# A hybrid decoder block on one core: gate and up products made ahead are looked up by the main loop, and the end of the mixing stage is reordered

## The chip, the cores and the metric

One core of one Trainium2 chip runs the whole block in one launch. The metric is device microseconds (us) of a run. All data is float32. A matrix product in full precision is made of three matmuls here: each operand is split into a rounded part and the rest, and three of the four cross products are added in PSUM.

## What is computed

The reference is one residual layer with two halves. The part that matters here, cut from it:

```
x = x + gt_m * (concat(attention(h), mlstm(h)) @ w_out)      # h = modulate(rms_norm(x))
h = modulate(rms_norm(x, g_ffn), sh_f, sc_f)
x = x + gt_f * ((silu(h @ w_gate) * (h @ w_up)) @ w_down)    # 1024 tokens, width 1024, D_FF = 2816
```

## The kernel before

The program is written as one long list of operations, and a scheduler fixes each engine's order when it is built. Its stages are: loads and norms ("init", "start"), the input projection ("vm", "min"), a stage with the attention and the output projection w_out ("at", "mm"), the gate and up projections ("gu"), and the down projection ("dn"). PE is TensorE, DVE VectorE, ACT ScalarE, POOL GpSimd, SP the queue that issues the DMAs.

**Gate and up.** D_FF is cut into 22 slices of 128. A pass f of the loop over slices makes the gate and the up result of one slice for all 1024 tokens, by a 2x2 scheme with seven products P1 to P7 instead of eight. One product contracts half the width: 4 tiles of 128, three matmuls each, 12 matmuls of 128x128 by 128x512, in `mm3_on` (L1052, L1053, L1054). So a pass has 84. P1 (weights: first half of the gate slice, operand A11) goes to a PSUM bank "g" and is copied out by ACT (L1138, into `q[:, 0]`); P2 (second half, operand A12) is added to it in the same bank, which gives the gate result, and ACT takes its silu into `q[:, 1]`. The five others go to banks "s" (`gu_pss`) and "t" (`gu_pst`). Their weights are sums of gate and up weights: `weights` makes them on POOL from two loaded buffers `rawgu` (L1115 t1, L1116 t2, L1121 t3, L1125 t4), and every product's weights are then split by ACT (the cast L242) and DVE (the subtract L243) into `gu_wt`, of which there are seven buffers. There are two buffers `rawgu`, so the pair for the next slice is loaded when the pair before has been read. The operands A22, S1 to S4 are sums over the normed tokens, made once by `sums` on DVE and POOL.

**Products made ahead.** A11 and A12 need only one half of the tokens each to be ready, so P1 and P2 of the slices 0 to 5 are made already while the attention stage ends (`first_two`, weights by `gate_weights` L1068): 144 matmuls, named `mm_psg<-mm_slab,mm_slab` or `mm_psg<-mm_slab,mm_s` with the lines L1052 to L1054 in the trace. Each result pair q is put in a dictionary `early`. The loop is meant to find it there. But `early` is a name of the enclosing function, and the same function binds it a second time before the stage runs, to the list of later token projections:

```
early = {}                                       # with first_two
...
early = [tok_body(...) for w in LATER.split()]   # L1351
...
        if f not in early:                       # weights, L1112, and gate_up
            got["P1"] = parts(g[:, 0])
```

The inner functions look the name up when they run. They find a list of seven entries: `early[f] = q` stores into it, and no slice number f is ever found in it. So the loop makes P1 and P2 again for all 22 slices.

**The end of the attention stage.** `drive` interleaves three streams, the projections "mm", the attention "at" and its inputs "qn", by rates. The last entry of "mm" is `tail`: the output projection of the column groups 2 and 3 (attention; 4 to 7 are the mLSTM heads) for the first half of the tokens (`last_out`, half 0), the norm and the transposition of that half (`h2_half`, L1004 on PE, L1005 on ACT), the weights and products of slices 0 and 1; then, when the attention's last results are there, the output projection for the second half of the tokens (groups 0 to 3, L155 to L157; L952 adds it to the residual), its norm and transposition, the other products ahead, and `sums`. The PSUM of this stage has two banks "g" and three "t".

**POOL's other work.** In even passes, `down_sums` (L1172 to L1176, four sums on POOL) makes sums of w_down and stores them for the down stage; in odd passes, `spill` (L1184 to L1187, four sums on POOL, seven stores) stores the results of two passes. Buffers of one size, the slabs, serve nearly everything; there are 39 (`NSLAB`).

Of the kernel before, what the change touches and what calls it, by code (L numbers as in the profile page):

```python
# [44 lines left out]
WM, WA, WL, WQ, R2 = 220, 140, 66, 28, 1.2  # L45
GA = (0, 0, 2, 3, 9, 18, 22, 24)

DOWN_AHEAD = 5
TWICE = 8
# [16 lines left out]
def hymba_block(ctx, tc, x, vecs, gate_bias, w_in, w_out, w_gu, w_down, w_ada_m, w_ada, b_ada,  # L66
# [1000 lines left out]
    def gate_weights(fs, tile=None):  # L1067

        for f in fs:
            got = []  # L1070
            raw = raws.tile([P, 2, HALF], F32, tag="raw", name=f"rawg{f}")
            nc.sync.dma_start(raw, w_gu[f, :, 0].rearrange("p (k n) -> p k n", k=2))
            h, l = ((tile or slab)([2, 4, P], FR) for _ in range(2))
            split(h.rearrange("p a k n -> p a (k n)"), l.rearrange("p a k n -> p a (k n)"), raw)
            gates_w[f] = [[(h[:, a, i], l[:, a, i]) for i in range(4)] for a in range(2)]

# [24 lines left out]
    def weights(pool, f, raw):  # L1101

        g, u = raw
        tt = nc.gpsimd.tensor_tensor

        def parts(src):
            w = work(pool, "wt", [2, 4, P], FR, bufs=7)
            split(w[:, 0].rearrange("p k n -> p (k n)"), w[:, 1].rearrange("p k n -> p (k n)"), src)
            return [(w[:, 0, i], w[:, 1, i]) for i in range(4)]

        got = {}
        if f not in early:  # L1112
            got["P1"] = parts(g[:, 0])
        t1, t2, t3 = (work(pool, "tr", [HALF], bufs=3) for _ in range(3))
        tt(t1, u[:, 0], g[:, 0], op=OP.subtract)  # L1115
        tt(t2, u[:, 1], t1, op=OP.subtract)  # L1116
        got["P6"] = parts(t2)
        got["P5"] = parts(t1)
        if f not in early:
            got["P2"] = parts(g[:, 1])  # L1120
        tt(t3, u[:, 1], u[:, 0], op=OP.subtract)  # L1121
        got["P7"] = parts(t3)
        got["P3"] = parts(u[:, 1])
        t4 = work(pool, "tr", [HALF], bufs=3)
# [192 lines left out]
    def tail(pool):  # L1317
# [30 lines left out]
    with tc.tile_pool(name="awork", bufs=1) as pool:  # L1348
        btab = slab([T])
        nc.sync.dma_start(btab, mask_tab)  # L1350
        early = [tok_body(("qk" if w[0] == "q" else "va") + w[1], raw_qk if w[0] == "q" else raw_v, int(w[1]),  # L1351
                          tuple(int(hf) for hf in w[2:])) for w in LATER.split()]
        items = early + [w_out_body([4, 5], (0, 1), True, ()), w_out_body([6, 7], (0,), False, ()),
# [8 lines left out]
        drive(("mm", after(chain(items), tail(pool)), WM), ("at", after(*att), WA), ("qn", after(*pre), WQ))  # L1362
        tick(99)
    open_psum("psum_f", s=3, t=2)
    with tc.tile_pool(name="fwork", bufs=1) as pool:
        lab[0] = "gu"
        raw = load_gu(0)
        w = weights(pool, 0, raw)
        for f in range(NF):
# [10 lines left out]
            else:  # L1380
                down_sums(f // 2)
# [77 lines left out]
```

## Time and profile before

| | |
|---|---|
| median of 3 runs | 1355.57 us (1353.12 to 1358.3) |
| the profiled execution | 1357.78 us, its span 1355.6 us |
| mean granted TensorE clock over the span | 0.988 |
| PE busy | 1306.1 us, 96% of the span |
| DVE, ACT, POOL busy | 65%, 43%, 40% |

The time of an execution is its span, from the first to the last instruction in the trace, and the little that lies around it, here 2.2 us. A matmul's row shows its start and its modelled length; matmuls overlap, so the distance of two starts is what one costs, not its length. An idle time in brackets stands in the row of the instruction that came after it, with the engine and line that ended it. The granted clock is given as a share of full speed.

### The profile page before, as it was taken

The page shows a single profiled execution, that of the slowest core. Times are in us where ns is not written, and L with a number is a line of the kernel's source. Part 1 is how long each engine was busy: PE and PEld are TensorE (multiplying, and loading weights), DVE is VectorE, ACT ScalarE, POOL GpSimd, SP SyncE. Part 2 cuts the span into 40 slices and gives each one's busy share as a digit, 9 for nine tenths or more (in the row PEclk, how much of TensorE's full clock was granted, in tenths as well). Part 3 has the DMA queues.
Part 4 walks back from the last instruction along what each step waited for, and adds up shares of the span by engine and source line. Part 5 has one row for each costly group of instructions (what it writes and reads, how often), then busy time and mean ns, then how long its engine had stood idle before and what let it go on. Part 6 is the DMA issues. An engine that isn't in the chain of part 4 may idle for free.

```text
span 1355.6 us, 18979 instructions
## 1 busy us (share of the span) xinstructions
PE 1306.1 (96%) x6983; PEld 1093.5 (81%) x6983; DVE 879.2 (65%) x1465; ACT 581.3 (43%) x1098; POOL 536.2 (40%) x417
## 2 busy tenths in 40 slices
PE   5999999999999999996979999999999999999998
PEld 5897888899899877775767888888888888888886
DVE  6837956973666698994367565556665555665575
ACT  5423444444565565556253233333332333644341
POOL 5401301333333385411154666766676573002121
PEclk9899999999999999997999999999999999999999
DMA  9134223532121132111112444344445436927564
GB/s 367 65 105 140 66 91 102 163 126 69 41 63 32 48 113 90 32 62 63 63 63 101 163 163 148 142 169 163 151 154 176 149 141 224 387 103 246 197 233 140
DMA packets 68579, 180.07 MB, mean 133 GB/s; under 512 B 7620, under 2 KB 7876, under 8 KB 68486
## 3 DMA queue, kind: packets, MB, share of 16 engines
q1 hardware_dynamic: 68486, 178.85, 38.3%
q8 instruction: 55, 0.90, 0.3%
q14 instruction: 38, 0.31, 0.1%
HBM read 138.72 MB, written 40.11 MB: 132 GB/s over the span
## 4 chain that ended last, share of the span: by engine, by line
PE 86%; DVE 6%; ACT 3%; issue 2%; DMA 2%; POOL 1%; SPq 0%; ACTq 0%; DVEq 0%; POOLq 0%
PE gu_pss L1053 6%; PE gu_pss L1054 6%; PE gu_pss L1052 6%; PE mm_psg L155 4%; PE mm_psg L156 4%; PE mm_psg L157 4%; PE min_psg L157 4%; PE min_psg L156 4%; PE min_psg L155 4%; PE gu_psg L1054 3%; PE gu_psg L1053 3%; PE gu_psg L1052 3%; PE at_psv L835 2%; PE at_pss L800 2%; PE dn_pss L1052 2%; PE dn_pss L1054 2%
## 5 line engine op out<-in xcount | busy, mean ns | idle before, releaser
L243 DVE TENSOR_TENSOR gu_wt<-gu_tr,gu_wt 128x512 fp32r<-128x512 f32 x88 | 87.3, 1011 | 88.6 <-ACT gu_wt L242 88.2
L1053 PE MATMUL gu_pss<-mm_slab,gu_wt 128*128 128x512 f32 x352 | 139.9, 397 | 3.6 <-DVE mm_slab L243 3.6
L1054 PE MATMUL gu_pss<-mm_slab,gu_wt 128*128 128x512 f32 x352 | 139.3, 396 | 0.0
L1052 PE MATMUL gu_pss<-mm_slab,gu_wt 128*128 128x512 f32 x352 | 138.6, 394 | 0.0
L242 ACT CAST gu_wt<-gu_tr 128x512 fp32r<-128x512 f32 x88 | 54.5, 622 | 189.4 <-POOL gu_tr L1116 107.4
L243 DVE TENSOR_TENSOR gu_wt<-rawgu,gu_wt 128x512 fp32r<-128x512 f32 x66 | 71.8, 1088 | 34.4 <-ACT gu_wt L242 34.2
L243 DVE TENSOR_TENSOR dn_wt<-dn_slab,dn_wt 128x512 fp32r<-128x512 f32 x72 | 53.1, 737 | 48.4 <-ACT dn_wt L242 47.2
L1053 PEld LDWEIGHTS gu_pss<-mm_slab,gu_wt 128*128 128x128 f32 x352 | 66.6, 189 | 21.1 <-DVE mm_slab L243 5.7
L157 PE MATMUL min_psg<-start_slab,min_slab 128*128 128x512 f32 x192 | 78.2, 407 | 0.8 <-DVE min_slab L243 0.8
L1052 PEld LDWEIGHTS gu_pss<-mm_slab,gu_wt 128*128 128x128 f32 x352 | 66.5, 189 | 15.5
L1054 PEld LDWEIGHTS gu_pss<-mm_slab,gu_wt 128*128 128x128 f32 x352 | 66.5, 189 | 15.1
L155 PE MATMUL min_psg<-start_slab,min_slab 128*128 128x512 f32 x192 | 77.1, 402 | 0.0
L156 PE MATMUL min_psg<-start_slab,min_slab 128*128 128x512 f32 x192 | 77.1, 402 | 0.0
L242 ACT CAST dn_wt<-dn_slab 128x512 fp32r<-128x512 f32 x72 | 44.7, 621 | 69.3 <-PE dn_pss L1054 29.4
L1245 POOL TENSOR_TENSOR dn_slab<-dn_slab,dn_slab 128x512 f32<-128x512 f32 x12 | 17.8, 1499 | 140.2 <-DVE dn_slab L1244 139.5
L156 PE MATMUL mm_psg<-mm_slab,start_slab 128*128 128x256 f32 x256 | 73.1, 286 | 0.0
L157 PE MATMUL mm_psg<-mm_slab,start_slab 128*128 128x256 f32 x256 | 73.0, 286 | 0.0
L155 PE MATMUL mm_psg<-mm_slab,start_slab 128*128 128x256 f32 x256 | 72.9, 286 | 0.0
L1053 PE MATMUL gu_psg<-mm_slab,gu_wt 128*128 128x512 f32 x176 | 69.4, 394 | 0.0
L1054 PE MATMUL gu_psg<-mm_slab,gu_wt 128*128 128x512 f32 x176 | 69.4, 394 | 0.0
L1052 PE MATMUL gu_psg<-mm_slab,gu_wt 128*128 128x512 f32 x176 | 69.2, 393 | 0.0
L809 ACT ACTIVATE at_s<-at_s,at_mins 128x128 f32<-128x128 f32 (+7 forms) x64 | 49.4, 777 | 41.6 <-DVE at_mins L803 21.0
(377 smaller groups left out, 3972.0 us busy)
## 6 DMA issues: line engine op xcount, KB each, us to landing
rawgu<-in_w_gu_dram SPq DMA_DIRECT2D x44, 512.0 KB, 4.4
pd<-gu_slab SPq DMA_DIRECT2D x77, 256.0 KB, 2.1
dn_slab<-pd SPq DMA_DIRECT2D x72, 256.0 KB, 5.3
ada_slab<-in_w_ada_dram SPq DMA_DIRECT2D x32, 512.0 KB, 4.4
gu_slab<-in_w_down_dram SPq DMA_DIRECT2D x22, 512.0 KB, 6.3
td<-gu_slab SPq DMA_DIRECT2D x22, 512.0 KB, 2.6
dn_slab<-td SPq DMA_DIRECT2D x44, 256.0 KB, 5.4
init_slab<-in_w_ada_m_dram SPq DMA_DIRECT2D x16, 512.0 KB, 10.2
```

Of the source, the lines that this page charges most:

```text
L155: mm(o, a[0], b[0], start=start, stop=False)
L156: mm(o, a[0], b[1], start=False, stop=False)
L157: mm(o, a[1], b[0], start=False, stop=stop)
L242: nc.scalar.copy(dst_h, src)
L243: (eng or nc.vector).tensor_tensor(dst_l, src, dst_h.bitcast(F32), op=OP.subtract)
L800: mm(o[:, e, 0:w], q[r, qi, cols], k[ch][r, ki, 0:w], start=qi == ki, stop=qi > ki)
L809: nc.scalar.activation(s[e][:, 0:n], s[e][:, 0:n], AF.Exp, bias=mins[e][:, 0:1], scale=-1.0, accum_out=z)
L835: mm(pv[:, e, P if short else 0:256], v[kb // 4][:, kb % 4, e, :], h[:, j * 256:j * 256 + (P if short else 256)], start=kb == 0 and i == 0 ...
L1052: mm(o, a[0], b[0], start=start, stop=False, skip_group_check=more)
L1053: mm(o, a[0], b[1], start=False, stop=False, skip_group_check=more)
L1054: mm(o, a[1], b[0], start=False, stop=stop, skip_group_check=more)
L1245: nc.gpsimd.tensor_tensor(y, y, xr, op=OP.add)
```

## The change

The diff, nearly whole. The list of projections gets a name of its own, so that `early` stays the dictionary. `FIRST` is 6: for slices under 6 `weights` makes no parts for P1 and P2, and `gate_up` takes q out of `early`.

```diff
-WM, WA, WL, WQ, R2 = 220, 140, 66, 28, 1.2
+WM, WA, WL, WQ, R2 = 220, 140, 66, 28, 1.1
+FIRST = 6
...
-    def gate_weights(fs, tile=None):
+    def gate_weights(fs):
         for f in fs:
...
-            h, l = ((tile or slab)([2, 4, P], FR) for _ in range(2))
+            h, l = (slab([2, 4, P], FR) for _ in range(2))
...
+            yield 0.05
...
-        if f not in early:
+        if f >= FIRST:
             got["P1"] = parts(g[:, 0])
...
-        if f not in early:
+        if f >= FIRST:
             got["P2"] = parts(g[:, 1])
...
-    def tail(pool):
+    all4 = [0, 1, 2, 3]
+
+    def tail():
 
         ws = w_out_load([2, 3])()()
         kept.update(ws)
-        w67 = {k: kept.pop(k) for k in (6, 7)}
-        yield from last_out([2, 3], ws, 0, ((2, 0), (3, 0)), (rest(w67),))
-        gate_weights((0, 1))
-        begun, rest_ = first_two((0, 1)), [first_two((2, 3)), first_two((4, 5))]
-        all4 = [0, 1, 2, 3]
-        wait = tuple((p, 1) for p in range(4))
-        while not all(v in done for v in wait):
+        yield from rest({k: kept.pop(k) for k in (6, 7)})
+        yield from last_out([2, 3], ws, 0, ((2, 0), (3, 0)), (gate_weights((0, 1)),))
+        while not all((p, 1) in done for p in range(4)):
             yield next(begun, None)
-        gate_weights((2, 3), lambda shape, dt: work(pool, "s", shape, dt, bufs=NS))
-        left = next(begun, None)
-        if left is None:
-            begun = rest_.pop(0)
-        yield from last_out(all4, {k: kept.pop(k) for k in all4}, 1, (), (begun,))
-        gate_weights((4, 5))
-        for g in rest_:
-            yield from g
+
+    begun = None
+
+    def second_half(pool):
+        w = {}
+
+        def ahead():
+            for _ in gate_weights((4, 5)):
+                pass
+            yield
+            w.update(weights(pool, 0, load_gu(0)))
+            yield
+
+        ws = {k: kept.pop(k) for k in all4}
+        tiles = w_out_tiles(all4, ws, 1, False)
+        for _ in gate_weights((2, 3)):
+            pass
+        bg.append(ahead())
+        xn = []
+        for t in tiles:
+            xn.append(normed(t))
+            tick()
+        for g in (begun, first_two((2, 3)), h2_half(1, xn), first_two((4, 5))):
+            for _ in g:
+                pass
         sums()
+        return w
...
-        early = [tok_body(...
+        later = [tok_body(...
...
+        begun = first_two((0, 1))
-        drive(("mm", after(chain(items), tail(pool)), WM), ("at", after(*att), WA), ("qn", after(*pre), WQ))
+        drive(("mm", after(chain(items), tail()), WM), ("at", after(*att), WA), ("qn", after(*pre), WQ))
         tick(99)
     open_psum("psum_f", s=3, t=2)
     with tc.tile_pool(name="fwork", bufs=1) as pool:
+        lab[0] = "mm"
+        w = second_half(pool)
         lab[0] = "gu"
-        raw = load_gu(0)
-        w = weights(pool, 0, raw)
+        summed = 0
         for f in range(NF):
...
             if f % 2:
                 spill(f // 2)
-            else:
-                down_sums(f // 2)
+            while f >= FIRST and summed * (NF - FIRST) < (f + 1 - FIRST) * (NF // 2):
+                down_sums(summed)
+                summed += 1
```

In words: the projection tiles of the groups 6 and 7 for the second half (48 matmuls) come before the last projection of the first half instead of behind it; the gate weights of slices 0 and 1 are made inside the norm of that half; the last output projection runs after the attention stage is closed, with the next stage's PSUM (three banks "s", two "t" instead of three "t"), followed by the products of slices 2 and 3, the transposition of the second half, the products of slices 4 and 5, and the sums; the weights of slice 0 are made while that projection runs. The sums of w_down, one set in each even pass before, are made in 11 of the 16 passes from f = 6 on: 6, 7, 8, 10, 11, 13, 14, 16, 17, 19, 20.

Three places show how the engines' orders move. In the changed file the lines after L47 stand two further down (L1052 is L1054 there, L1004 is L1006).

PE where the attention stage ends, before: the last transpositions of the first half of the tokens, then the first product ahead (slice 0, one bank).

```order
L1004 MATMUL mm_pst_6841<-ident,mm_slab_6415 128x128
L1004 MATMUL mm_pst_6841<-ident,mm_slab_6473 128x128
L1004 MATMUL mm_pst_6841<-ident,mm_slab_6537 128x128
L1052 MATMUL mm_psg_6877<-mm_slab_6793,mm_slab_6855 128x512
L1053 MATMUL mm_psg_6877<-mm_slab_6793,mm_slab_6855 128x512
L1054 MATMUL mm_psg_6877<-mm_slab_6793,mm_slab_6856 128x512
L1052 MATMUL mm_psg_6877<-mm_slab_6811,mm_slab_6855 128x512
```

The same place after:

```order
L1006 MATMUL mm_pst_6757<-ident,mm_slab_6668 128x128
L1054 MATMUL mm_psg_6833<-mm_slab_6733,mm_slab_6707 128x512
L1054 MATMUL mm_psg_6872<-mm_slab_6733,mm_slab_6713 128x512
L1055 MATMUL mm_psg_6833<-mm_slab_6733,mm_slab_6707 128x512
L1056 MATMUL mm_psg_6833<-mm_slab_6733,mm_slab_6708 128x512
L1055 MATMUL mm_psg_6872<-mm_slab_6733,mm_slab_6713 128x512
L1056 MATMUL mm_psg_6872<-mm_slab_6733,mm_slab_6714 128x512
L1006 MATMUL mm_pst_6763<-ident,mm_slab_6503 128x128
L1006 MATMUL mm_pst_6763<-ident,mm_slab_6559 128x128
L1006 MATMUL mm_pst_6763<-ident,mm_slab_6618 128x128
```

Before, all transpositions came first and the products of slice 0 alone followed. After, the products of two slices (banks 6833 and 6872) stand between the transpositions, tile by tile; the attention's last transpositions and readout (L824, L837) come after them.

ACT in a pass of the loop, before (slice 1): copy of P1, seven weight casts, copy of P5, two silu.

```order
L1138 COPY gu_slab_7534<-gu_psg_7535 128x512
L242 CAST gu_wt_7637<-rawgu_0_7530 128x512
L1146 COPY gu_slab_7550<-gu_pss_7566 128x512
L1063 ACTIVATE gu_slab_7534<-gu_psg_7535 128x512
L242 CAST gu_wt_7645<-gu_tr_7641 128x512
L242 CAST gu_wt_7648<-gu_tr_7640 128x512
L242 CAST gu_wt_7651<-rawgu_0_7530 128x512
L242 CAST gu_wt_7655<-gu_tr_7642 128x512
L242 CAST gu_wt_7658<-rawgu_1_7532 128x512
L242 CAST gu_wt_7663<-gu_tr_7661 128x512
L1063 ACTIVATE gu_slab_7550<-gu_slab_7550 128x512
```

A pass after (slice 2):

```order
L244 CAST gu_wt_7679<-gu_tr_7675 128x512
L244 CAST gu_wt_7682<-gu_tr_7674 128x512
L244 CAST gu_wt_7686<-gu_tr_7676 128x512
L1148 COPY gu_slab_7600<-gu_pss_7616 128x512
L244 CAST gu_wt_7689<-rawgu_1_7597 128x512
L244 CAST gu_wt_7694<-gu_tr_7692 128x512
L1065 ACTIVATE gu_slab_7600<-gu_slab_7600 128x512
```

In the passes 0 to 5 the copy and the silu of the bank "g" and the two casts from the first buffer `rawgu_0` are gone. On PE the products of `gu_psg` go from 528 matmuls to 384 over the whole loop, so 144 fewer; the products ahead stay 144. POOL and SP have as many instructions as before.

POOL in one pass, before, from the sum behind P7 of slice 1 to that of slice 2 (L1152 marks a pass): the spill of the slices 0 and 1 among the weight sums t1 to t4; the first sum of `down_sums` comes in the next pass, behind the last row.

```order
L1115 TENSOR_TENSOR gu_tr_7789<-rawgu_1_7681,rawgu_0_7679 128x512
L1185 TENSOR_TENSOR gu_slab_7667<-gu_slab_7551,gu_slab_7666 128x512
L1186 TENSOR_TENSOR gu_slab_7666<-gu_slab_7405,gu_slab_7551 128x512
L1116 TENSOR_TENSOR gu_tr_7790<-rawgu_1_7681,gu_tr_7789 128x512
L1121 TENSOR_TENSOR gu_tr_7791<-rawgu_1_7681 128x512
L1187 TENSOR_TENSOR gu_slab_7667<-gu_slab_7551,gu_slab_7667 128x512
L1125 TENSOR_TENSOR gu_tr_7810<-rawgu_0_7679,gu_tr_7790 128x512
L1152 TENSOR_TENSOR gu_slab_7700<-gu_slab_7698,gu_slab_7699 128x512
L1172 TENSOR_TENSOR gu_slab_7815<-gu_slab_7815 128x512
L1173 TENSOR_TENSOR gu_slab_7815<-gu_slab_7816,gu_slab_7815 128x512
```

After, a pass with both, shown from its third row to its end (L1154, slice 6) and one row on:

```order
L1187 TENSOR_TENSOR gu_slab_8318<-gu_slab_8202,gu_slab_8317 128x512
L1188 TENSOR_TENSOR gu_slab_8317<-gu_slab_8056,gu_slab_8202 128x512
L1118 TENSOR_TENSOR gu_tr_8451<-rawgu_1_8342,gu_tr_8450 128x512
L1123 TENSOR_TENSOR gu_tr_8452<-rawgu_1_8342 128x512
L1189 TENSOR_TENSOR gu_slab_8318<-gu_slab_8202,gu_slab_8318 128x512
L1174 TENSOR_TENSOR gu_slab_8330<-gu_slab_8330 128x512
L1127 TENSOR_TENSOR gu_tr_8471<-rawgu_0_8340,gu_tr_8451 128x512
L1175 TENSOR_TENSOR gu_slab_8330<-gu_slab_8331,gu_slab_8330 128x512
L1177 TENSOR_TENSOR gu_slab_8331<-gu_slab_8331,gu_slab_8330 128x512
L1178 TENSOR_TENSOR gu_slab_8331<-gu_slab_8331 128x512
L1154 TENSOR_TENSOR gu_slab_8361<-gu_slab_8359,gu_slab_8360 128x512
L1174 TENSOR_TENSOR gu_slab_8476<-gu_slab_8476 128x512
```

Before, four sums of the spill or four of `down_sums` stood in a pass beside its own five, nine in all. After, the four of `down_sums` (now L1174, L1175, L1177, L1178) and the four of the spill (L1186 to L1189, the first just ahead of the rows shown) stand in one, thirteen in all, and one of them goes ahead of t4 (L1127).

## Rows read from the trace of the kernel before

**Rows 1.** The page: span, and busy time of two engines.

```profile
span 1355.6 us, 18979 instructions
PE 1306.1 (96%) x6983; PEld 1093.5 (81%) x6983; DVE 879.2 (65%) x1465; ACT 581.3 (43%) x1098; POOL 536.2 (40%) x417
```

**Rows 2.** Busy us by stretch: PE, PEld, DVE, ACT, POOL, clock, DMA share, GB/s.

```profile
620.00:630.00 10.00, 3.49 (x17) 1.83 (x15) 6.63 (x11) 9.66 (x16) 0.00 (x0) 0.83 0.00 1
630.00:640.00 10.00, 6.32 (x16) 4.74 (x16) 3.58 (x3) 4.83 (x8) 1.68 (x2) 0.67 0.54 166
...
700.00:710.00 10.00, 7.23 (x31) 5.22 (x29) 10.00 (x9) 7.55 (x15) 8.69 (x6) 1.00 0.30 105
...
1000.00:1020.00 20.00, 20.00 (x88) 16.22 (x88) 13.79 (x15) 6.23 (x11) 14.35 (x10) 1.00 0.42 164
```

**Rows 3.** Line L1052 by tile: count, duration ns min/median/max, first and last start.

```profile
L1052 PE MATMUL gu_psg<-mm_slab,gu_wt x176: 388/393/402, 703.1 to 1128.2; 128*128 128x512 f32 x176
...
L1052 PE MATMUL mm_psg<-mm_slab,mm_slab x32: 389/395/795, 628.8 to 702.2; 128*128 128x512 f32 x32
...
L1052 PE MATMUL mm_psg<-mm_slab,mm_s x16: 388/393/796, 670.1 to 691.1; 128*128 128x512 f32 x16
```

**Rows 4.** Timeline of PE, products ahead at full clock: start, length, what.

```profile
691.77 0.40 PE L1052 MATMUL mm_psg<-mm_slab,mm_slab 128*128 128x512 f32 x1
...
702.63 0.39 PE L1054 MATMUL mm_psg<-mm_slab,mm_slab 128*128 128x512 f32 x1
```

**Rows 5.** Timeline of PE, idle times in brackets, end of the attention stage.

```profile
621.41 1.32 PE L1004 MATMUL mm_pst<-ident,mm_slab 128*128 128x128 f32 x8 [1.10 <-ACT mm_slab L1005]
623.78 0.66 PE L1004 MATMUL mm_pst<-ident,mm_slab 128*128 128x128 f32 x4 [1.05 <-ACT mm_slab L1005]
628.79 0.80 PE L1052 MATMUL mm_psg<-mm_slab,mm_slab 128*128 128x512 f32 x1 [4.35 <-ACT mm_slab L242]
...
637.77 0.79 PE L1052 MATMUL mm_psg<-mm_slab,mm_slab 128*128 128x512 f32 x1 [3.65 <-ACT mm_slab L1085]
...
638.79 0.63 PE L1054 MATMUL mm_psg<-mm_slab,mm_slab 128*128 128x512 f32 x1
639.22 0.63 PE L1052 MATMUL mm_psg<-mm_slab,mm_slab 128*128 128x512 f32 x1
```

**Rows 6.** The same view, from the second half's transpositions into the loop.

```profile
684.58 0.80 PE L1052 MATMUL mm_psg<-mm_slab,mm_s 128*128 128x512 f32 x1 [3.51 <-ACT mm_slab L1085]
...
706.70 0.50 PE L1053 MATMUL gu_pss<-mm_slab,gu_wt 128*128 128x512 f32 x1 [0.67 <-DVE mm_slab L243]
...
710.08 0.50 PE L1053 MATMUL gu_pss<-mm_slab,gu_wt 128*128 128x512 f32 x1 [2.18 <-DVE mm_slab L243]
...
711.78 0.77 PE L1053 MATMUL gu_pss<-mm_slab,gu_wt 128*128 128x512 f32 x1 [0.74 <-DVE mm_slab L243]
```

**Rows 7.** Timeline of ACT before the first product ahead, and at its copy.

```profile
625.31 1.46 ACT L1005 ACTIVATE mm_slab<-mm_pst,modf 128x512 f32<-128x512 f32 x2
...
627.67 2.01 ACT L242 CAST mm_slab<-rawg 128x1024 fp32r<-128x1024 f32 x2
...
633.91 1.04 ACT L242 CAST mm_s<-rawg 128x1024 fp32r<-128x1024 f32 x1 [4.23 <-DMA rawg<-in_w_gu_dram]
```

**Rows 8.** Timeline of DVE: one split with POOL idle, one beside POOL.

```profile
999.34 0.69 DVE L243 TENSOR_TENSOR gu_wt<-rawgu,gu_wt 128x512 fp32r<-128x512 f32 x1
...
1002.11 1.81 DVE L243 TENSOR_TENSOR gu_wt<-gu_tr,gu_wt 128x512 fp32r<-128x512 f32 x1
```

**Rows 9.** Groups of instructions, 640 to 1100 us: busy us, mean ns, idle and releaser.

```profile
L1125 POOL TENSOR_TENSOR gu_tr<-rawgu,gu_tr 128x512 f32<-128x512 f32 x21 | 30.7, 1460 | 33.5 <-DVE gu_wt L243 33.5
...
L243 DVE TENSOR_TENSOR mm_slab<-mm_slab,mm_slab 128x512 fp32r<-128x512 f32 x20 | 16.6, 901 | 0.0
```

**Rows 10.** The page's DMA issues: count, KB each, us to landing.

```profile
rawgu<-in_w_gu_dram SPq DMA_DIRECT2D x44, 512.0 KB, 4.4
pd<-gu_slab SPq DMA_DIRECT2D x77, 256.0 KB, 2.1
```

More of the change, by code (lines that the diff above doesn't have):

```diff
@@ L1065, in hymba_block @@
     gates_w = {}
-    def gate_weights(fs, tile=None):
+    def gate_weights(fs):
         for f in fs:
-            got = []
             raw = raws.tile([P, 2, HALF], F32, tag="raw", name=f"rawg{f}")
             nc.sync.dma_start(raw, w_gu[f, :, 0].rearrange("p (k n) -> p k n", k=2))
-            h, l = ((tile or slab)([2, 4, P], FR) for _ in range(2))
+            h, l = (slab([2, 4, P], FR) for _ in range(2))
             split(h.rearrange("p a k n -> p a (k n)"), l.rearrange("p a k n -> p a (k n)"), raw)
             gates_w[f] = [[(h[:, a, i], l[:, a, i]) for i in range(4)] for a in range(2)]
+            yield 0.05
     def first_two(fs):
@@ L1315, in rest @@
             yield 2.6
-    def tail(pool):
+    all4 = [0, 1, 2, 3]
+    def tail():
         ws = w_out_load([2, 3])()()
         kept.update(ws)
-        w67 = {k: kept.pop(k) for k in (6, 7)}
-        yield from last_out([2, 3], ws, 0, ((2, 0), (3, 0)), (rest(w67),))
-        gate_weights((0, 1))
-        begun, rest_ = first_two((0, 1)), [first_two((2, 3)), first_two((4, 5))]
-        all4 = [0, 1, 2, 3]
-        wait = tuple((p, 1) for p in range(4))
-        while not all(v in done for v in wait):
-            yield next(begun, None)
-        gate_weights((2, 3), lambda shape, dt: work(pool, "s", shape, dt, bufs=NS))
-        left = next(begun, None)
-        if left is None:
-            begun = rest_.pop(0)
-        yield from last_out(all4, {k: kept.pop(k) for k in all4}, 1, (), (begun,))
-        gate_weights((4, 5))
-        for g in rest_:
-            yield from g
+        yield from rest({k: kept.pop(k) for k in (6, 7)})
+        yield from last_out([2, 3], ws, 0, ((2, 0), (3, 0)), (gate_weights((0, 1)),))
+        while not all((p, 1) in done for p in range(4)):
+            yield next(begun, None)
+    begun = None
+    def second_half(pool):
+        halves = lambda shape, dt: slab(shape, dt)
+        w = {}
[17 more added lines that the diff above has]
+                pass
         sums()
+        return w
     with tc.tile_pool(name="mwork", bufs=1) as pool:
@@ L1350, in hymba_block @@
         nc.sync.dma_start(btab, mask_tab)
-        early = [tok_body(("qk" if w[0] == "q" else "va") + w[1], raw_qk if w[0] == "q" else raw_v, int(w[1]),
+        later = [tok_body(("qk" if w[0] == "q" else "va") + w[1], raw_qk if w[0] == "q" else raw_v, int(w[1]),
                           tuple(int(hf) for hf in w[2:])) for w in LATER.split()]
-        items = early + [w_out_body([4, 5], (0, 1), True, ()), w_out_body([6, 7], (0,), False, ()),
+        items = later + [w_out_body([4, 5], (0, 1), True, ()), w_out_body([6, 7], (0,), False, ()),
                          w_out_body([0, 1], (0,), False, ((0, 0), (1, 0)))]
```

## The prediction

> **What bounds the kernel now.** I read the page first: TensorE is busy for 1306.1 of the span's 1355.6 us [rows 1], so a change gains by taking matmuls away or by closing PE's idle times, and loses by opening new ones. Then the table of windows: from about 717 us on PE is full to the end (20.00 of 20.00 in the stretch shown, clock 1.00), while DVE and POOL are at some 14 of 20 [rows 2]. Only the end of the attention stage, about 620 to 717 us, has holes: PE works 3.49 and 6.32 of 10 us there, at a granted clock of 0.83 and 0.67 [rows 2]. Last the timeline of PE for those holes and what ends them [rows 5, 6]. A matmul's price is the distance of two starts: 47 steps from 691.77 to 702.63 us, so 0.231 us [rows 4]. A pass of 84 costs 19.4 us, one of 60 costs 13.9.
>
> **1. Six pairs of products are no longer made twice.** The trace shows both makings: 48 matmuls of each of the three lines ahead (32 and 16), and then 176 of each in the loop, which is 22 passes times 8 [rows 3]. After the change the first are looked up, and the loop makes 16 passes times 8: 3 lines x 48 = 144 matmuls go, from a stretch that is full. 144 x 0.231 = **33.3 us**. What goes with them on ACT and DVE (six copies, six silu, twelve casts, twelve subtracts) ran beside PE and is priced at nothing.
>
> The Trainium skill, page "TensorE: Matmul & The Clock Gate", section "Wait — 56ns, not 53.3ns?", gives 215.7 ns from start to start for 512 columns on the warm array; by that the term would be 31.1 us and the forecast 2 us later. The measured 0.231 us decides here: it already holds whatever the three-matmul pattern adds in this kernel.
>
> **2. The attention's end is filled.** Before, PE waited 1.10 + 1.05 + 4.35 + 3.65 = 10.2 us between 620 and 638 us [rows 5]. The first three belong to one chain: ACT copies and casts eight tiles and then two gate weights (0.73 us a copy, 1.0 a weight cast, busy 9.66 of 10 us [rows 2, 7]) before any product ahead can start. The fourth is the copy L1085 between slice 0's two products, standing on ACT behind a weight cast that waits 4.23 us for its DMA [rows 7]. Behind the two long waits the matmuls start 0.43 us apart (638.79, 639.22 [rows 5]), half the full rate (1.2 of 2.4 GHz), 10 and 13 of them, 0.2 us too much each: 4.6 us. Together 14.8 us. After, the weights of slices 0 and 1 are cast ahead of the copies, the 48 products of two slices lie between the transpositions, and the attention's last readout lies behind them; there are two banks, so no product waits for the copy of the other. ACT's part of that place is about 15 us (8 copies, 8 casts, 4 attention casts, 2 weights), and PE has 48 x 0.231 = 11 us of products beside the readout. What stays open is the first tile's copy, cast and split, about 2.3 us (0.73 + 0.6 + 0.9 [rows 7, 9]), one or two steps like the 1.10 and 1.05, and some half-rate matmuls: I take 5.5 us, so **9.3 us** gained. Bounds: 0 (the wait moves to the interleaved products) and 14.8.
>
> **3. The way into the loop is traded.** Before, PE lost 3.51 + 0.67 + 2.18 + 0.74 = 7.1 us there [rows 6] and 16 half-rate matmuls (eight each behind the 3.51 and the 0.74), 3.2 us: 10.3. The 3.51 is the copy between two products of one bank again; the others are DVE, full from 700 to 710 us [rows 2], late with the splits of the operand sums (20 of them, 0.90 us each, with 8 sums [rows 9]). After, the loop starts with P6, which needs such a sum at once, and P1 and P2, 24 matmuls of cover, are gone; between the last transposition and the first sum's product lie 24 matmuls instead of 72. So I expect a short stop before S2, and one of about 4 us before the first A22 product, the last operand that DVE delivers; two transposition banks instead of three cost up to 0.7 us each time ACT's copy is late. Against this, the copy between two products goes, and the weights of slice 0 come earlier. I take 8.6 us lost: **1.7 us** gained, with bounds of 5 lost and 8 gained.
>
> **4. Moved work.** The weight loads of slices 0, 2 to 5 (4.4 us each to landing [rows 10]) start under the last output projection, 96 matmuls or 22 us, which covers them. The rate 1.1 for 1.2 alters only which filler stands where and is priced at nothing; if that cover fails it shows inside term 2. In passes 0 to 5, 13.9 us long, POOL has 5 sums, with a spill 9, and DVE five splits: little is spare but nothing is above the pass, 1 us taken. From slice 6 on, POOL has 13 sums in the passes 7, 11, 13, 17 and 19. One takes 1.43 us in the dense stretch (14.35 for 10 [rows 2]), so 18.7 of 19.4 us: it fits, with nothing to spare for waits such as those for the split before t4 (33.5 us in 21 [rows 9]). On SP the load of the next pair is queued behind the stores of those sums, which wait for the fourth; its 4.4 us lie beside the pass's products. The passes between have 5 or 9 sums, and seven weight buffers give a lead. I take 3 us, bounds 0 and 18 (rival B): **4 us** lost.
>
> **Sum.** 1357.8 - 33.3 - 9.3 - 1.7 + 4 = 1317.5 for an execution like the profiled one; that stood 2.2 us above the median, so the forecast for the median is **1315 us**. Its own range is 1304 (terms 2 and 3 at 19 together, term 4 at 1) to 1322 (8 and 8).
>
> **Rivals.**
> B, the port between DVE and POOL. A split takes 0.69 us alone and 1.81 beside a POOL sum [rows 8], as if it stood still until the sum is through. If the two exclude each other, a pass with 13 POOL sums (1.29 us each undisturbed) and nine two-input DVE operations (0.69) needs 13 x 1.29 + 9 x 0.69 = 23.0 us against 19.4; five such passes cost 18 us, 1330 us in all. Against it: the passes of 9 sums need 17.8, so some is caught up. The Trainium skill, page "SBUF — State Buffer", section "Who interferes with whom", says just that: a DVE instruction with two SBUF inputs contends with a GpSimd instruction that reads SBUF, and who starts first has the port for the whole instruction. The durations in rows 8 agree; the rule speaks against gathering the sums of w_down into fewer passes. Chance 0.14.
> A, the pair of raw weights in short passes. One pair at a time: load 4.4, four sums at 1.46, P7's sum, four spill sums, and the split waited for (1.6), in a row 4.4 + 9 x 1.46 + 1.6 = 19.1 us with a spill and 13.3 without, mean 16.2 against 13.9: 2.3 x 6 = 14 us, 1328. Against it: the spill's sums and the load overlap. Chance 0.07.
> C, the transition gains nothing: terms 2 and 3 come out at 0, because the missing cover opens waits as long as those closed: 1326. Chance 0.10.
> D, slabs. The 28 operands, the row of gt and six waiting results hold 35 of 39 slabs as the loop begins; a pass takes three, and a spill two more, which come free when seven stores (2.1 us each to landing [rows 10]) have landed. If DVE's write into such a slab waits in its queue, the splits behind it wait too, and the short passes stop. To end slower than 0.5% above before, 1362 us, it must cost 8 us in each of the six, 22 us a pass where 13.9 are needed; standing for 8 of the 14.7 us that seven stores take one behind the other would do it, 1364 us. Against it: the stores are issued one pass before the slab is wanted. Chance 0.06, half of it slower, half within 0.5%.
> That the lookup still finds nothing is out: the order has 384 matmuls of `gu_psg`, not 528.
>
> **How the numbers follow.** The forecast's case has 0.63, B 0.14, C 0.10, A 0.07, D 0.06. Taking the range from 1304 to 1331 holds the first four but their tails. 0.5% is 6.8 us, what a measurement of this kernel can tell from no change; all cases but D lie below 1348.8, so faster 0.94, within 0.5% 0.03, slower 0.03.
>
> **What would show it.** Right: 128 `gu_psg` matmuls on each of the three lines; P6 first in passes 0 to 5, pst products some 13.9 us apart there; PE's idle at 620 to 640 us down to about 5 us; a wait on the splits of A22 early in the first pass; no PE idle after some 700 us. Wrong: PE rows in the loop with idle ended by `gu_wt` splits (A or B, by whether the chain goes on to POOL's sums or to the DMA of `rawgu`), DVE waiting on DMAs of `pd` (D), or as many us lost before the loop as before (C). A term 1 other than 33 would mean that the start distance is not the price of a matmul.

## The result and the profile after

The changed kernel took 1315.06 us, the median of 4 runs (1313.2 to 1316.92), against 1355.2 us before (1353.12 to 1358.3): a ratio of 0.9702, 95% interval 0.9679 to 0.9725. The forecast was 1315, with 1304 to 1331 around it. The profiled execution took 1313.2 us, its span 1311.3; so the spans differ by 44.3 us, where the medians differ by 40, and what follows adds up to the former. Two names are used below: the short passes are the passes 0 to 5, which now have 60 matmuls and take 13.9 us on PE; the packed passes are those in which POOL now has 13 sums (7, 11, 13, 17 and 19).

The page of the changed kernel, the lines that answer to [rows 1]:

```profile
span 1311.3 us, 18583 instructions
PE 1267.0 (97%) x6839; PEld 1059.3 (81%) x6839; DVE 872.4 (67%) x1453; ACT 568.0 (43%) x1074; POOL 540.8 (41%) x417
```

PE has 144 matmuls fewer. The line that they left, by tile, as in [rows 3] (count, duration min/median/max, first and last start):

```profile
L1054 PE MATMUL gu_psg<-mm_slab,gu_wt x128: 387/393/402, 774.4 to 1084.3; 128*128 128x512 f32 x128
...
L1054 PE MATMUL mm_psg<-mm_slab,mm_slab x32: 388/396/793, 615.4 to 670.5; 128*128 128x512 f32 x32
```

128 in place of 176, and the first of them 774 us into the span: the passes 0 to 5 have none. The stretches of [rows 2] (busy us of PE, PEld, DVE, ACT, POOL, clock, DMA):

```profile
610.00:620.00 10.00, 8.24 (x43) 6.48 (x44) 6.61 (x9) 9.63 (x16) 0.73 (x2) 0.83 0.48 155
620.00:630.00 10.00, 10.00 (x63) 8.69 (x61) 6.35 (x10) 8.04 (x15) 0.00 (x0) 1.00 0.01 5
680.00:690.00 10.00, 7.34 (x32) 5.23 (x30) 10.00 (x7) 6.66 (x13) 9.93 (x6) 1.00 0.00 0
690.00:700.00 10.00, 9.39 (x33) 7.21 (x33) 10.00 (x17) 8.45 (x17) 0.00 (x0) 0.83 0.00 0
750.00:760.00 10.00, 7.43 (x30) 5.67 (x29) 5.53 (x6) 2.11 (x4) 8.13 (x6) 0.93 0.30 115
1000.00:1020.00 20.00, 20.00 (x88) 16.22 (x87) 11.80 (x14) 6.29 (x12) 12.71 (x10) 1.00 0.43 155
```

The place where PE worked 3.49 and 6.32 of 10 us is filled (8.24 and 10.00; it lies 10 us earlier now); ACT is as full there as it was, but PE has other work beside it. The way into the loop still has its hole, with DVE full, and there is a new one at 750 us. The waits themselves, from PE's timeline (start, length, instruction, idle before it and what ended it):

```profile
612.98 0.55 PE L1006 MATMUL mm_pst<-ident,mm_slab 128*128 128x128 f32 x3 [0.76 <-DVE mm_slab L989]
614.18 1.44 PE L1006 MATMUL mm_pst<-ident,mm_slab 128*128 128x128 f32 x8 [0.65 <-ACT mm_slab L1007]
...
659.03 0.50 PE L1054 MATMUL mm_psg<-mm_slab,mm_slab 128*128 128x512 f32 x1 [1.52 <-DVE mm_slab L954]
...
681.04 0.50 PE L1054 MATMUL mm_psg<-mm_slab,ada_slab 128*128 128x512 f32 x1 [0.68 <-ACT mm_slab L1087]
688.84 0.50 PE L1055 MATMUL gu_pss<-mm_slab,ada_wt 128*128 128x512 f32 x1 [1.78 <-DVE mm_slab L245]
690.53 0.79 PE L1055 MATMUL gu_pss<-mm_slab,ada_wt 128*128 128x512 f32 x1 [0.74 <-DVE mm_slab L245]
700.16 0.50 PE L1055 MATMUL gu_pst<-mm_slab,ada_wt 128*128 128x512 f32 x1 [0.23 <-DVE mm_slab L245]
758.52 0.74 PE L1054 MATMUL gu_pss<-mm_slab,gu_wt 128*128 128x512 f32 x1 [2.57 <-DVE gu_slab L1145]
...
776.66 0.50 PE L1054 MATMUL gu_pss<-mm_slab,gu_wt 128*128 128x512 f32 x1 [1.68 <-DVE gu_slab L1145]
```

Three groups: the attention's end (0.76 + 0.65), the way into the loop (1.52 + 0.68 + 1.78 + 0.74 + 0.23, and 0.43 not shown), and two waits in the short passes (2.57 + 1.68). Three waits of 0.34 to 0.61 us between 610 and 641 us, 1.5 us in all, are left aside. After 777 us PE waits no more. How the last two come about is seen on POOL and DVE, first POOL:

```profile
706.91 1.47 POOL L1117 TENSOR_TENSOR gu_tr<-rawgu,rawgu 128x512 f32<-128x512 f32 x1 [16.98 <-DMA rawgu<-in_w_gu_dram]
...
744.86 1.61 POOL L1127 TENSOR_TENSOR gu_tr<-rawgu,gu_tr 128x512 f32<-128x512 f32 x1 [1.29 <-DVE gu_wt L245]
751.87 1.29 POOL L1117 TENSOR_TENSOR gu_tr<-rawgu,rawgu 128x512 f32<-128x512 f32 x1 [5.40 <-DMA rawgu<-in_w_gu_dram]
753.12 1.28 POOL L1154 TENSOR_TENSOR gu_slab<-gu_slab,gu_slab 128x512 f32<-128x512 f32 x1
...
770.72 1.79 POOL L1117 TENSOR_TENSOR gu_tr<-rawgu,rawgu 128x512 f32<-128x512 f32 x1 [3.19 <-DMA rawgu<-in_w_gu_dram]
```

and DVE in the same pass:

```profile
754.44 1.75 DVE L1162 TENSOR_TENSOR gu_slab<-gu_slab,gu_slab 128x512 f32<-128x512 f32 x1 [5.26 <-POOL gu_slab L1154]
756.11 0.68 DVE L1156 TENSOR_TENSOR gu_slab<-gu_pss,gu_slab 128x512 f32<-128x512 f32 x1
...
757.78 0.68 DVE L1145 TENSOR_TENSOR gu_slab<-gu_pss,mm_slab 128x512 f32<-128x512 f32 x1
```

t4 (L1127) frees the raw buffers, the next pair takes 5.4 us to land, t1 (L1117) waits for it, and the sum behind P7 (L1154) stands behind t1 on POOL. DVE's L1162 waits for that sum, with the evictions L1156 and L1145 behind it, and PE for the bank that L1145 empties.

### The profile page after: what moved, and what is told of

Its sections match the earlier page's. It is cut to its first block, busy times and chain, and to the rows that moved or that the text cites. A ratio compares the mean times of both kernels' runs of the same rounds, so it can differ in the third digit from the quotient of the medians.

```text
span 1311.3 us, 18583 instructions
## 1 busy us (share of the span) xinstructions
PE 1267.0 (97%) x6839; PEld 1059.3 (81%) x6839; DVE 872.4 (67%) x1453; ACT 568.0 (43%) x1074; POOL 540.8 (41%) x417
## 4 chain that ended last, share of the span: by engine, by line
PE 80%; DVE 9%; DMA 4%; ACT 3%; issue 2%; POOL 2%; SPq 0%; POOLq 0%; DVEq 0%; ACTq 0%
PE gu_pss L1055 5%; PE gu_pss L1054 5%; PE gu_pss L1056 5%; PE mm_psg L157 4%; PE mm_psg L158 4%; PE min_psg L159 4%; PE mm_psg L159 4%; PE min_psg L158 4%; PE min_psg L157 4%; PE at_psv L837 2%; DMA rawgu<-in_w_gu_dram 2%; PE gu_psg L1056 2%; PE gu_psg L1055 2%; PE at_pss L802 2%; PE gu_psg L1054 2%
## 5 line engine op out<-in xcount | busy, mean ns | idle before, releaser
L1054 PE MATMUL gu_pss<-mm_slab,gu_wt 128*128 128x512 f32 x336 | 133.0, 397 | 4.3 <-DVE gu_slab L1145 4.3
L1055 PE MATMUL gu_pss<-mm_slab,gu_wt 128*128 128x512 f32 x336 | 133.6, 398 | 0.0
L1056 PE MATMUL gu_pss<-mm_slab,gu_wt 128*128 128x512 f32 x336 | 132.9, 396 | 0.0
L244 ACT CAST gu_wt<-gu_tr 128x512 fp32r<-128x512 f32 x84 | 51.3, 621 | 169.3 <-POOL gu_tr L1118 111.6
L1054 PEld LDWEIGHTS gu_pss<-mm_slab,gu_wt 128*128 128x128 f32 x336 | 63.7, 190 | 20.9 <-DVE gu_slab L1145 5.1
L1056 PEld LDWEIGHTS gu_pss<-mm_slab,gu_wt 128*128 128x128 f32 x336 | 63.8, 190 | 14.6
L1055 PEld LDWEIGHTS gu_pss<-mm_slab,gu_wt 128*128 128x128 f32 x336 | 63.6, 189 | 14.6
L245 DVE TENSOR_TENSOR gu_wt<-rawgu,gu_wt 128x512 fp32r<-128x512 f32 x53 | 57.5, 1084 | 17.4 <-ACT gu_wt L244 17.4
L805 DVE CUSTOM_DVE_ANT_0 at_s<-at_pss,mo_slab 128x512 f32<-128x512 f32 (+3 forms) x96 | 49.4, 551 | 20.4 <-PE at_pss L802 19.6
L245 DVE TENSOR_TENSOR dn_slab<-dn_slab,dn_slab 128x512 fp32r<-128x512 f32 x72 | 53.2, 740 | 12.9 <-ACT dn_slab L244 12.9
L244 ACT CAST at_th<-at_pst 128x512 fp32r<-128x512 f32 (+1 forms) x80 | 41.8, 546 | 44.6 <-PE at_psv L837 36.2
```

The source lines that it names most:

```text
L244: nc.scalar.copy(dst_h, src)
L245: (eng or nc.vector).tensor_tensor(dst_l, src, dst_h.bitcast(F32), op=OP.subtract)
L805: nc.vector.tensor_tensor_reduce(s[e][:, ch * 512:ch * 512 + w], o[:, e, 0:w], btab[:, b0:b0 + w], 1.0, 3e38, OP.add, OP.min, mins[e][:, c ...
L1054: mm(o, a[0], b[0], start=start, stop=False, skip_group_check=more)
L1055: mm(o, a[0], b[1], start=False, stop=False, skip_group_check=more)
L1056: mm(o, a[1], b[0], start=False, stop=stop, skip_group_check=more)
```

## The experiments

All ratios are to the kernel before, run beside each. Where a run is compared with the change in us, the two medians come from different sessions, in which the kernel before took 1355.2 to 1356.1 us.

**The lookup alone.** The kernel before, with the list renamed and nothing else:

```diff
-        early = [tok_body(...
+        later = [tok_body(...
```

> The kernel before with nothing but the second binding of the name removed, so that the lookup works; the old order of the attention stage and the old places of the sums of w_down stay. Theory (the gain is first of all the 144 matmuls, 33.3 us of a full TensorE, and the reordering gave some 10 us beside): 1355 - 33 = 1322 us, plus up to 6 us because the loop's first products lose 24 matmuls of cover and the short passes wait for the raw pair as they do in the changed kernel, so 1322 to 1328. In its trace 128 gu_psg matmuls on each line, the waits of 4.35, 3.65 and 3.51 us still there. Rival (the repeated products cost less than their number, because DVE and POOL need the time anyway, and the new order is what pays): 1335 us or more.

Measured: 1341.02 us, ratio 0.9892 (0.9871 to 0.9913). The theory missed, and the time lies in the rival's range: 128 `gu_psg` matmuls a line, 33 us of products gone, and only 15 us won. The waits at the attention's end were as before; the lost 18 us are new or longer waits on the way into the loop and in it (21.2 us of waits from 650 us on, 7.4 before), with half-rate matmuls behind some. PE's timeline shows these among others, ended by the splits and evictions on DVE and ACT:

```profile
703.44 0.50 PE L1053 MATMUL gu_pss<-mm_slab,gu_wt 128*128 128x512 f32 x1 [2.57 <-DVE mm_slab L243]
706.81 0.79 PE L1053 MATMUL gu_pss<-mm_slab,gu_wt 128*128 128x512 f32 x1 [2.19 <-DVE mm_slab L243]
...
724.00 0.50 PE L1052 MATMUL gu_pst<-mm_slab,gu_wt 128*128 128x512 f32 x1 [1.92 <-ACT gu_wt L242]
752.79 0.50 PE L1054 MATMUL gu_pss<-mm_slab,gu_wt 128*128 128x512 f32 x1 [1.87 <-DVE gu_wt L243]
...
792.36 0.47 PE L1052 MATMUL gu_pss<-mm_slab,gu_wt 128*128 128x512 f32 x1 [1.92 <-DVE gu_slab L1151]
...
819.06 0.49 PE L1052 MATMUL gu_pss<-mm_slab,gu_wt 128*128 128x512 f32 x1 [1.91 <-DVE gu_slab L1143]
```

**The rest without the lookup.** The changed kernel, with P1 and P2 made for all slices:

```diff
-        if f in early:
-            q = early.pop(f)
+        if False:
+            q = None
...
-        if f >= FIRST:
+        if True:
```

> The changed kernel with the lookup undone: P1 and P2 of the slices 0 to 5 are made again in the loop, all else as changed. Theory: 1315 + 33 for the 144 matmuls, less the 5 us that the changed kernel loses by PE waits in passes 3 to 5 (no short passes here) and less up to 3 us at the loop's start (P1 covers the first sum's split): 1340 to 1344 us. Rival as in the run before it: if the repeated products cost less than their number, 1330 us or less.

Measured: 1345.49 us, ratio 0.9927 (0.99 to 0.9955), a little above the expectation; the rival, 1330 us or less, fell. All of the change but the lookup gives 10.6 us against the 1356.1 of that session (6 to 14 by the interval); the lookup on top of it gives 30.4 (1345.5 to 1315.1), the lookup in the old kernel 15.

**The sums of w_down back in the even passes**, in the changed kernel:

```diff
-            while f >= FIRST and summed * (NF - FIRST) < (f + 1 - FIRST) * (NF // 2):
-                down_sums(summed)
-                summed += 1
+            else:
+                down_sums(f // 2)
```

> The changed kernel with the sums of w_down back in every even pass. Theory: the 13 sums in one pass cost nothing in the changed kernel (no PE wait after 780 us), while in passes 0, 2 and 4 four more sums on GpSimd come before the weight sums of a short pass: the two waits of 2.57 and 1.68 us grow or get company, 1316 to 1322 us. Rival (the prediction's: the packed passes cost about 3 us and the short ones 1): 1311 to 1314 us.

Measured: 1321.02 us, ratio 0.9737 (0.9719 to 0.9755), 6 us slower than the change, as the theory had it; the prediction's split, 3 us for the packed passes and 1 for the short ones, was the rival here and fell. PE waits in nearly every short pass, and the first two shown are for weights:

```profile
730.79 0.47 PE L1054 MATMUL gu_pss<-mm_slab,gu_wt 128*128 128x512 f32 x1 [1.58 <-ACT gu_wt L244]
733.45 0.50 PE L1056 MATMUL gu_pss<-mm_slab,gu_wt 128*128 128x512 f32 x1 [1.95 <-DVE gu_wt L245]
...
773.36 0.47 PE L1054 MATMUL gu_pss<-mm_slab,gu_wt 128*128 128x512 f32 x1 [1.89 <-DVE gu_slab L1153]
```

**The sum behind P7 on VectorE** in the passes 0 to 5:

```diff
-        nc.gpsimd.tensor_tensor(o[:, 1], r[:, 1], z[:, 0], op=add)
+        (tt if f < FIRST else nc.gpsimd.tensor_tensor)(o[:, 1], r[:, 1], z[:, 0], op=add)
```

> The changed kernel with the sum behind P7 of the slices 0 to 5 on VectorE instead of GpSimd. Theory (in passes 3 and 5 that sum stands on GpSimd behind t1, which waits 5.4 us for the raw pair; VectorE's next operation waits for it, and the PSUM bank that PE wants is behind that): both PE waits, 4.3 us with about 1.3 us of half-rate matmuls behind them, go: 1309 to 1311 us. Rival (the raw pair itself sets the pace of the short passes): PE waits as long, then for the weights' splits: 1314 to 1316 us.

Measured: 1315.77 us, ratio 0.9705 (0.9685 to 0.9726). The theory of the queue fell, and the time lies in the rival's range: the wait at 758 us shrinks to 0.15, and the next one grows to 4.40, again for a bank that DVE empties and not, as the rival had it, for the weights' splits. POOL's t1 still waits for the raw pair.

```profile
777.15 0.80 PE L1054 MATMUL gu_pss<-mm_slab,gu_wt 128*128 128x512 f32 x1 [4.40 <-DVE gu_slab L1145]
```

and on POOL

```profile
770.67 1.66 POOL L1117 TENSOR_TENSOR gu_tr<-rawgu,rawgu 128x512 f32<-128x512 f32 x1 [6.26 <-DMA rawgu<-in_w_gu_dram]
```

The chain shown above is the way in which the lag reaches PE, not its cause; closing that way makes PE wait a pass later.

**No loads for the slices 1 to 5:**

```diff
+        if 0 < f < FIRST:
+            return resident[0]
```

> The changed kernel, but the raw weights of the slices 1 to 5 are not loaded: the pair of slice 0 stays and is used for them (so five slices are made of the wrong weights; ten loads of 512 KB are left out, nothing else). Theory (in the short passes the one raw pair sets the pace: load about 5 us, then its sums, then the next load; measured 17.6 and 14.9 us from one t4 to the next where a pass has 13.9): without the loads both PE waits in the passes 3 to 5 go, 4.3 us with 1.3 us of half rate: 1309 to 1311 us. Rival (DVE and POOL stand in each other's way, the loads do not matter): the waits stay, 1314 to 1316 us.

Measured: 1310.05 us, ratio 0.9667 (0.965 to 0.9684), 5.0 us under the change. The two intervals touch at their ends (0.9679 to 0.9684), but all four runs here (1308.33 to 1312.46) lie below the four of the change (1313.2 to 1316.92). Between 705 and 800 us one wait is left:

```profile
771.47 0.50 PE L1054 MATMUL gu_pss<-mm_slab,gu_wt 128*128 128x512 f32 x1 [0.43 <-DVE gu_slab L1150]
```

So the loads of the raw pair set the pace of the short passes; DVE and POOL do the same sums here without holding PE up.

**The lookup and the late sums, on the old order** (the kernel before with the rename and the `while` of the change):

> The kernel before with the lookup mended, as in the first experiment, and with the sums of w_down moved to the passes from 6 on as in the change; only the new order of the attention's end is missing. Theory (from the run with the sums back in the even passes, 6 us slower than the change, and from the lookup alone, where PE waits 12 us in passes 1 to 5): 1341 less some 8 to 10 us, 1331 to 1333 us. Rival (the waits of the short passes come from the late start of the old order, not from the sums): 1338 us or more.

Measured: 1335.71 us, ratio 0.9853 (0.9835 to 0.9871), between the two. The late sums give 5.3 us here, close to the 6 of the run with the sums back, and the rest of the change, the new order of the attention's end above all, 20.6 on top (to 1315.1), twice what all but the lookup gives without it (10.6). Much of that difference lies on the way into the loop: this run waits there for 12.6 us in six pieces, three of which stand here, while the change waits 5.4.

```profile
683.24 0.80 PE L1052 MATMUL mm_psg<-mm_slab,mm_s 128*128 128x512 f32 x1 [3.51 <-ACT mm_slab L1085]
...
704.39 0.50 PE L1053 MATMUL gu_pss<-mm_slab,gu_wt 128*128 128x512 f32 x1 [2.57 <-DVE mm_slab L243]
707.77 0.79 PE L1053 MATMUL gu_pss<-mm_slab,gu_wt 128*128 128x512 f32 x1 [2.19 <-DVE mm_slab L243]
```

**A third raw buffer, one slab given up** (`NSLAB` 38; every third raw half goes to a buffer of the loop's own pool):

> The changed kernel with a third buffer for raw weights in the loop, for which one of the 39 slabs is given up. Theory (raw pair): the first half of the next pair is loaded a pass early, so the load after t4 is one of 512 KB instead of two, some 2 us a pass less; the PE waits in passes 3 to 5 shrink to 1 or 2 us: 1311 to 1313 us, if a slab less costs nothing. Rival (sums and splits set the pace): 1314 to 1316 us. If slabs are short: slower, with DVE or POOL waiting for stores.

Measured: 1321.02 us, ratio 0.9744 (0.9725 to 0.9764). Slower, as the last case had it. No wait is left between 715 and 800 us, though PE also waits longer on the way into the loop here (8.3 us, 5.4 in the change), which gives the loads more time. But the attention stage is late: the eight transpositions that start at 614.18 us in the change start here at

```profile
624.69 1.32 PE L1006 MATMUL mm_pst<-ident,mm_slab 128*128 128x128 f32 x8 [0.65 <-ACT mm_slab L1007]
```

So one slab of 39 costs 10 us before the loop; the waits of PE there are ended by DVE and ACT, and no wait of DVE, ACT or POOL there by a store, which is what the expectation had named. That the third buffer gives some of this back in the loop fits the missing waits, but the run does not part the two.

**Three of the four sums of the early spills on VectorE:**

```diff
+        if 2 * i < FIRST:
+            tt = nc.vector.tensor_tensor
```

> The changed kernel with three of the four sums of the spills of slices 0 to 5 on VectorE instead of GpSimd. Theory (raw pair): the way from one t4 to the next in odd passes, 17.6 us, loses up to three sums of 1.7 us and falls below the pass of 13.9; PE's waits of 2.57 and 1.68 us go: 1310 to 1312 us. Rival (VectorE's own queue is the limit there): it now has three operations more, and PE waits longer for L1145: 1316 to 1319 us.

Measured: 1314.36 us, ratio 0.9698 (0.9684 to 0.9712): no gain, neither range was met, and the waits are still there (1.69, 2.81 and 0.52 us). In the odd pass t4 now waits for DVE's split, so the way from one t4 to the next stays at 17.9 us:

```profile
762.38 1.60 POOL L1127 TENSOR_TENSOR gu_tr<-rawgu,gu_tr 128x512 f32<-128x512 f32 x1 [3.70 <-DVE gu_wt L245]
```

Beside the run without loads this says that moving sums from POOL to DVE does not help while the load stays.

**The gate weights behind the transpositions:**

```diff
-        yield from last_out([2, 3], ws, 0, ((2, 0), (3, 0)), (gate_weights((0, 1)),))
+        yield from last_out([2, 3], ws, 0, ((2, 0), (3, 0)))
+        for _ in gate_weights((0, 1)):
+            pass
```

> The changed kernel with the gate weights of slices 0 and 1 loaded and split behind the transpositions of the first half, as before the change, instead of inside that projection. Theory (the 4.35 us wait of before was ACT's copies and casts, with the weight casts last; what closed it is that the weights are ready when the first tile is): PE waits 2 to 4 us again before the first product ahead, with some half-rate matmuls: 1317 to 1320 us. Rival (the attention's readout behind it is what fills PE): 1314 to 1316 us.

Measured: 1319.37 us, ratio 0.9737 (0.9721 to 0.9753): 4.3 us slower, as the theory had it (the intervals touch at 0.9721 to 0.9725, the single runs do not). PE's granted clock in 620 to 630 us is 0.77 instead of 1.00, and small waits for ACT stand between the transpositions, the first being

```profile
618.55 1.97 PE L1006 MATMUL mm_pst<-ident,mm_slab 128*128 128x128 f32 x8 [1.05 <-ACT mm_slab L1007]
```

The 4.35 us do not come back; the attention's last transpositions and readout stand there now. So the early weights account for some 4.3 of the 12 us that this hole gave back; that the readout gives the rest is argued from the order, no run leaves it out.

**More cover before the loop:** the products of slices 2 and 3 behind the transposition.

```diff
-        for g in (begun, first_two((2, 3)), h2_half(1, xn), first_two((4, 5))):
+        for g in (begun, h2_half(1, xn), first_two((2, 3)), first_two((4, 5))):
```

> The changed kernel with the products of slices 2 and 3 behind the transposition of the second half instead of ahead of it: 72 matmuls stand between the last transposition and the first product of the loop, as in the kernel before, instead of 24. Theory (the waits before the first S2 product, 1.78 and 0.74 us with 1.6 us of half rate behind them, are for want of cover over VectorE's sums and splits): they go, 4 us, but the transpositions come in a row with two banks and each waits some 0.4 us for ACT's copy, 2 to 3 us: 1312 to 1314 us. Rival (VectorE is full until A22 is split, so the wait only moves to a later operand): 1314 to 1317 us.

Measured: 1312.65 us, ratio 0.9692 (0.9673 to 0.971). The waits before S2 are gone, as expected. The transpositions cost more than expected, and for another reason: not a short wait at each copy but one of 5.35 us before the last 24. ACT's copy L1007, which ends it, stands behind two weight casts that wait for POOL:

```profile
673.11 5.48 PE L1006 MATMUL mm_pst<-ident,mm_slab 128*128 128x128 f32 x24 [5.35 <-ACT mm_slab L1007]
```

and on ACT

```profile
671.24 1.14 ACT L244 CAST gu_wt<-gu_tr 128x512 fp32r<-128x512 f32 x2 [5.83 <-POOL gu_tr L1118]
672.28 1.44 ACT L1007 ACTIVATE mm_slab<-mm_pst,modf 128x512 f32<-128x512 f32 x2
```

The profile is that of the slowest of the four runs (1316.01; the others took 1312.1 to 1313.0). The interval overlaps that of the change; whether it is faster is not settled.

**Quarters of the raw weights**, each loaded when its own readers are done:

```diff
+        for i, h in ((0, 0), (1, 0), (1, 1), (0, 1)):
+            nc.sync.dma_start(pair[i][:, h], w_gu[f, :, i, h * HALF:(h + 1) * HALF])
```

> The changed kernel with the raw weights of a slice loaded as four quarters of 256 KB into one fixed pair of buffers, in place of two halves into rotating ones: each quarter is loaded as soon as its own readers are done, so only the last one stands behind t4. Theory (raw pair): the way from t4 to the next t1 shrinks from about 5 us of load to nothing or little, the short passes keep their 13.9 us, and the PE waits of passes 3 to 5 go: 1309 to 1311 us. Rival (more DMAs on the same queue, each waiting in order behind the other, cost what is won): 1314 to 1318 us.

Measured: 1314.46 us, ratio 0.9703 (0.9677 to 0.9728): the theory missed, and the time lies in the rival's range, though what shows is not the queue's order: the wait has moved from t1 to t2 on POOL, whose quarter is free only when P3's weights have been split:

```profile
748.72 1.67 POOL L1119 TENSOR_TENSOR gu_tr<-rawgu,rawgu 128x512 f32<-128x512 f32 x1 [0.63 <-DVE gu_wt L245]
754.21 1.29 POOL L1120 TENSOR_TENSOR gu_tr<-rawgu,gu_tr 128x512 f32<-128x512 f32 x1 [3.81 <-DMA rawgu<-in_w_gu_dram]
```

**Both together:**

> The edits of the two runs before it together. If both theories hold, the gains add: 1307 to 1309 us. If the cover gains nothing, as e13 alone: 1309 to 1311 us.

Measured: 1313.39 us, ratio 0.9692 (0.9676 to 0.9708). About as the cover alone; the gains do not add, and neither range was met. None of these versions is clearly faster than the change.

## Why the prediction held, and where it did not

**Term 1, 33.3 us.** 144 matmuls fell out, as counted. Their 33.3 us are not won by the lookup itself: alone it gives 15, in the company of the rest 30.4. The step "priced at nothing" was about what goes with the products on ACT and DVE; what the prediction put into terms 3 and 4 is that the products were also cover for the weights of the loop. The prediction added the terms up as if each stood by itself; they do not. Of the 18 us that the lookup alone lost, the late sums give back 5.3, and the rest of the change some 10 (20.6 with the lookup, 10.6 without). That missing cover is what opened those waits is read from the rows of the first run; no run adds cover alone to the old order.

**Term 2, 9.3 us** for the attention's end: 14.8 us were lost there, now 0.76 + 0.65 of waits and six matmuls at half rate, 2.6 in all, so 12.2. That the attention's readout covers the first tile's chain, which I had left open, is argued. The change of the rate from 1.2 to 1.1 and the 48 matmuls moved ahead have no run of their own.

**Term 3, 1.7 us** for the way into the loop: 10.3 us before, now 5.4 of waits and eight half-rate matmuls, 1.6, so 7.0, and 3.3 won. The place was wrong: the 4 us at A22 are 0.23 (1.7 in the runs with the sums back, with P7's sum or the spill on VectorE, and with quarters), and the larger wait stands before S2, where I expected a short stop. The terms 2 and 3 as forecast, 11 together, agree with the 10.6 that all but the lookup gives, where no short pass interferes; the 15.5 read from the waits lies above the 14 that this run's interval allows, so the split between the terms is good to some us only.

**Term 4, 4 us lost:** right in size, wrong in place. I put 1 us on the short passes and 3 on the packed ones; measured are 4.25 us of waits and eight half-rate matmuls, 1.7, in the short passes, and none from slice 6 on. The failed step is "little is spare but nothing is above the pass". Rival A's sum was the better one: it had 16.2 us for a pair, and from t1 at 706.91 to t1 at 770.72 us four passes take 63.8, so 16.0 each, against 13.9. It cost 6 us instead of 14: the four cycles fall only 8.2 us behind, where the rival counted six, and that the weights made ahead took up the rest is argued. That the load is the cause is shown by the run without it (5.0 us less, with the same sums on both engines). Of the signs named, "no PE idle after some 700 us" did not come; the waits that came are ended by DVE's evictions, and go back to the DMA of `rawgu`, as named for A.

**The sum:** 33.3 + 12.2 + 3.3 - 6.0 = 42.8 of the 44.3 us between the spans; the other 1.5 is within the scatter of runs. That the median came out at 1315 is in part luck: terms 2 and 3 gave 4.5 us more than forecast and term 4 took 2.0 more, and single runs scatter by 4 us.

**Rival B** (the port) came to nothing in time, and its sum of 23.0 us is not borne out. The pass with 13 sums between two L1154 of POOL, in the changed kernel:

```profile
816.66 1.68 POOL L1154 TENSOR_TENSOR gu_slab<-gu_slab,gu_slab 128x512 f32<-128x512 f32 x1 [1.23 <-DVE gu_slab L1153]
...
841.13 1.76 POOL L1154 TENSOR_TENSOR gu_slab<-gu_slab,gu_slab 128x512 f32<-128x512 f32 x1
...
857.51 1.74 POOL L1154 TENSOR_TENSOR gu_slab<-gu_slab,gu_slab 128x512 f32<-128x512 f32 x1
```

24.5 us where PE's pass has 19.4, but 4.87 of them are a wait for the load, so the 13 sums take 19.6, not 23.0. The next pass has 16.4: POOL is 5 us late and has 3 of it back one pass later, and PE does not wait. "Some is caught up", the argument against the rival, held. **C** fell with terms 2 and 3. **D** fell: in the changed kernel no wait of PE, DVE or POOL in the short passes leads to a store. The run with 38 slabs shows that they are nevertheless just enough.

## What to carry to other kernels

Before work is taken off the bounding engine, ask what it covered: the same 144 matmuls were worth 15 us in one kernel and 30 in the other. When a pass gets shorter, work out the cycle of each buffer that is reloaded in it (here load, sums, splits, 16 us) and compare it with the new pass; here moving single sums to another engine did nothing, taking the load out did. A table that is filled in one place and looked up in another deserves a count of its hits.

## What the runs showed of the hardware

VectorE and GpSimd slow each other both ways. In the changed kernel GpSimd's sum L1154 takes 1.28 to 1.30 us in the four passes in which no VectorE operation with two inputs from SBUF runs beside it, and 1.67 to 1.79 us in the other 18. VectorE's L1162 takes 0.68 or 0.69 us in the 17 passes in which no GpSimd sum runs beside it, 1.75 to 1.78 us in four in which one does, and 0.94 in one where the two overlap by 0.39 us; two of its rows:

```profile
737.20 0.69 DVE L1162 TENSOR_TENSOR gu_slab<-gu_slab,gu_slab 128x512 f32<-128x512 f32 x1 [0.76 <-POOL gu_slab L1154]
...
754.44 1.75 DVE L1162 TENSOR_TENSOR gu_slab<-gu_slab,gu_slab 128x512 f32<-128x512 f32 x1 [5.26 <-POOL gu_slab L1154]
```

The Trainium skill, page "SBUF — State Buffer", section "Who interferes with whom", says that a VectorE operation with two SBUF inputs contends with a GpSimd operation that reads SBUF. The trace agrees; what the contention costs PE is not separated by any run.

The half rate of TensorE did not follow each wait: after 2.57 us, and after 1.78 and 0.74 close together, seven or eight matmuls started 0.43 us apart instead of 0.23, that is at 1.2 instead of 2.4 GHz; after a single 1.68 us none did.
